# Issuing 64-row matmuls in turns for two heads, one in each row half of the array, and laying out the PSUM pools anew

## The chip, the core and the metric

The kernel runs on one core of one Trainium2 chip. The metric is the device time of one execution in microseconds (us), as the median of several runs of the same program. TensorE is called PE here, VectorE DVE, ScalarE ACT, GpSimd POOL and SyncE SP, as the profile calls them.

## What is computed

Two layers of a decoder trunk on 512 positions with 1024 features. Each layer is a gated feed-forward block, a mixer and a second feed-forward block, each on a normalised and modulated input. The mixer projects its input once and runs three head groups on it: a gated linear recurrence (HGRN2), sparse attention whose keys an indexer selects, and a state-space scan (SSD). Cut to what matters here:

```python
def token_mixing(h, w_in, w_out, ...):
    (hq, hf, hi, hg, aq, ak, av, iq, ik, iw, sz, sxbc, sdt) = jnp.split(h @ w_in, offsets, axis=-1)
    o_a = hgrn2_mixer(hq, hf, hi, hg, lb, hg_norm_g)             # 4 heads of 64
    o_b = dsa_mixer(aq, ak, av, iq, ik, iw, kn_g, kn_b)          # 4 heads of 64, 8 index heads of 64
    o_c = mamba2_mixer(sz, sxbc, sdt, ...)                       # 8 heads of 64, state 128
    return jnp.concatenate([o_a, o_b, o_c], axis=-1) @ w_out

def dsa_mixer(...):                                              # for each block of 128 queries
    logits = jax.nn.relu(jnp.einsum('bthd,bsd->bths', qib, k_idx))
    score = jnp.einsum('bths,bth->bts', logits, wib)             # causal, future keys at -1e30
    _, sel = lax.top_k(score, n_keep)                            # n_keep = 128
    s = jnp.einsum('bthd,btkd->bhtk', qb, k_sel) * ATT_DIM ** -0.5
    return jnp.einsum('bhtk,btkd->bthd', jax.nn.softmax(s), v_sel)

def reference(x, c, ...):
    for l in range(2):
        x = x + 0.5 * g1 * swiglu(modulate(rms_norm(x)), w_ffn_gu[l, 0], w_ffn_down[l, 0])
        x = x + g2 * token_mixing(modulate(rms_norm(x)), w_in[l], w_out[l], ...)
        x = x + 0.5 * g3 * swiglu(modulate(rms_norm(x)), w_ffn_gu[l, 1], w_ffn_down[l, 1])
    return rms_norm(x, final_norm_g)
```

## The kernel before

The residual stream lies feature-major in eight tiles of 128 features by 512 positions. Large products are made in fp32r by splitting each operand into a high and a low part and adding three matmuls (`mm3`, L304 to L307); weights arrive by DMA in SP's queue as `wraw`, ACT makes the high part `whi` (L300) and DVE the low part `wlo` (L301). The two feed-forward blocks of a layer make gate and up products (`pg`, `pu`) per 128 hidden features, and then the down product `pd`.

The mixer (from L443) projects some outputs feature-major, as `pf` in `fm` (24 matmuls of 512 columns each), and others time-major, as `pt` in `tm_group` (96 matmuls of 256 columns for each of the groups `winV`, `winG`, `winC0`, `winC1`). Its parts are generators, which `zipped` (L729) advances in the order of positions given by hand (`ZD`, `ZH`, `ZQ`, `ZC`, `ZG`, `ZS`, `ZA`). The order on each engine is set when the kernel is built: a scheduler with a time model of its own moves instructions among those that are ready, by priority, where the pools have a free buffer. On the chip each engine runs its list in that order.

The parts that the change touches:
- `topk` (L536) makes the index scores. For each query block j from 1 to 3 and each of 8 index heads, a matmul `ipl` of 64 contracted rows (L543) goes through a relu on ACT (L545) and is added to `iacc` on DVE (L548, L550). Then 16 rounds of MAX8 (L559) and MATCH_REPLACE8 (L560) per block pick 128 keys.
- `attend(j)` (L743) takes each of the four heads in turn: score matmul `apl` of 64 rows (L750), softmax on DVE and ACT (L754 to L757), transposes `apt` (L761), a copy `pT` on ACT (L763), and the product with the values `apo` (L765).
- `hgrn` (L613) makes the diagonal `ldg` (L645) and seven levels of the chunk's scores. A level is two differences on DVE (L656, L657), an exponential on ACT (L658), two products on POOL (L659, L660), matmuls `lsc` of 64 rows (L667) and a COPY_PREDICATED into `asc` on DVE (L669). Then the states `hst` are carried over four blocks (`hps` L704, `hpo` L695 and L698).
- `ssd` follows with `pxs`, `pcb`, `prow`, `pyd`, `pst` and `pyo`, and the output product is `po` (L305 to L307 again), whose input `pyt` (L917) transposes.

A head of 64 features lies in rows 0 to 63 or 64 to 127 of its tile, so the matmuls of even heads use the upper half of the array's rows and those of odd heads the lower half. An fp32 matmul is two passes and has two records in the trace; a transpose has one.

[...] Before, `psmm` holds three buffers (`mm`, L70), and `pssm` holds three for `sm` (L73) and two for `hm` (L76), each of one bank:

```python
        pm = pool("psmm", 3, space=bass.MemoryType.PSUM)
        pq = pool("pssm", 2, space=bass.MemoryType.PSUM)
```

Of the kernel before, what the change touches and what calls it, by code (L numbers as in the profile page):

```python
# [11 lines left out]
F32 = mybir.dt.float32  # L12
# [6 lines left out]
P = 128  # L19
D = 1024  # L20
S = 512
# [33 lines left out]
def body(nc, tc, A):  # L55
    ctx = ExitStack()
    with ctx:
# [5 lines left out]
        pm = pool("psmm", 3, space=bass.MemoryType.PSUM)  # L63
        pq = pool("pssm", 2, space=bass.MemoryType.PSUM)
# [189 lines left out]
        def lead(l, i, ws, ps):  # L254
# [8 lines left out]
            pb = sm("pb", (P, 2))  # L263
            with tc.manual_schedule(engines={mybir.EngineType.PE}):
                for k, (xh, xl) in enumerate(ahead):
                    if k == KR[0]:
                        rs = rstd(range(NB), sm)
                    if k == KR[1]:
                        rb = act("C", "rb")
                        ACT.activation(rb, spread_rows(rs, sm), AF.Copy)  # L270
                    for (wh, wl, _), p in zip(ws, ps):
                        mm3(p, wh[:, blk(k)], wl[:, blk(k)], xh, xl, k == 0, k == NF - 1)
# [38 lines left out]
        def begin(pre):  # L311
            with tc.high_priority(0):
                for f in range(NF):
                    sumsq(f, tag="A", eng=V)
                rs = rstd(range(NB), hm)
                rb = act("A", "rb")
                ACT.activation(rb, spread_rows(rs, hm), AF.Copy)
# [10 lines left out]
                for step in SEQ:  # L328
# [11 lines left out]
                    else:  # L340
                        j = len(W)
                        pre[j] = mm("pg"), sm("pu")
# [22 lines left out]
        def ffn(l, w, side, nxt):  # L365
# [5 lines left out]
            else:  # L371
                pre[0] = mm("pg"), sm("pu")
                hh, hl, sb, rb = lead(l, i, [weights(A["wgu"][l, w, 0, g], 1024, True) for g in range(2)], pre[0])
            for hf in range(2):
                ah, al = [], []
                for jj in range(n):
# [3 lines left out]
                    else:  # L380
                        pg, pu = mm("pg"), sm("pu")
# [24 lines left out]
                for f in range(NF):  # L406
# [15 lines left out]
                    else:  # L422
                        with tc.manual_schedule(engines={mybir.EngineType.PE}):
# [5 lines left out]
                            rs = rstd((0, 1), sm)  # L429
                            down(half(1), KT[0], KT[1])  # L430
                            prb = spread_rows(rs, sm)
                            down(half(1), KT[1], n)
                            update(f, pd, gate, None, hf, half(1))
                            rs = rstd((2, 3), sm)
# [3 lines left out]
                            finish(half(1), spread_rows(rs, sm))  # L438
# [5 lines left out]
        def mixer(l, nxt):  # L444
# [68 lines left out]
            for src in (ik, ak):  # L513
# [10 lines left out]
                ps = sm("kTp")  # L524
# [11 lines left out]
            def topk():  # L536
                for j in range(1, NB):
                    n = (j + 1) * P
                    acc = act("A", "iacc")
                    for h in range(IH):  # L540
                        pl = sm("ipl")
                        ph = slice((h % 2) * 64, (h % 2) * 64 + 64)
                        PE.matmul(pl[:, :n], iqr[h // 2][ph, blk(j)], ikT[ph, :n], start=True, stop=True)  # L543
                        rl = act("A", "irl")
                        ACT.activation(rl[:, :n], pl[:, :n], AF.Relu)  # L545
                        w = iw[:, j, h:h + 1]
                        if h == 0:
                            V.tensor_scalar(acc[:, :n], rl[:, :n], w, None, op0=OP.mult)  # L548
                        else:
                            V.scalar_tensor_tensor(acc[:, :n], rl[:, :n], w, acc[:, :n], op0=OP.mult, op1=OP.add)  # L550
# [54 lines left out]

            def hgrn():
# [33 lines left out]
                for par in range(2):  # L640
                    for f in range(2):
                        ps = hm("ldg", (P, NB, P))
                        ph = slice(par * 64, par * 64 + 64)
                        for b in range(NB):
                            PE.matmul(ps[:, b], kf[f][ph, blk(b)], q[f][ph, blk(b)], start=True, stop=True)  # L645
                        V.tensor_tensor(Asc[par][f], ps, ident[:, None, :].to_broadcast([P, NB, P]), op=OP.mult)
                yield
                for li, m in enumerate(LEVELS):
# [13 lines left out]
                    for par in range(2):  # L662
                        ph = slice(par * 64, par * 64 + 64)
                        for f in range(2):
                            ps = hm("lsc")
                            for b in range(NB):
                                PE.matmul(ps[:, blk(b)], xl[f][ph, blk(b)], xl[f][ph, blk(b)],  # L667
                                          start=True, stop=True)
                            V.copy_predicated(v4(Asc[par][f].rearrange("p b t -> p (b t)"))[:, :, 1],  # L669
                                              masks[:, li].rearrange("p (g m) -> p g m", m=m), v4(ps)[:, :, 1])  # L670
                    yield
                kd = [act("B", "kd", shape=(P, NB, P)) for _ in range(2)]
                for f in range(2):
# [5 lines left out]
                    ps = hm("pkd", (P, NB, P))  # L679
# [10 lines left out]
                for b in range(NB):  # L690
                    po = hm("hpo", (P, 2, P))
# [9 lines left out]
                    if b < NB - 1:  # L701
                        for f in range(2):
                            pk = hm("hps", (P, P))
# [39 lines left out]
            def attend(j):  # L743
                n = (j + 1) * P
                po = sm("apo", (P, AH, 64))
                rsum = sp.tile([P, AH], F32, name="rsum")
                for h in range(AH):
                    ph = slice((h % 2) * 64, (h % 2) * 64 + 64)
                    pl = sm("apl")
                    PE.matmul(pl[:, :n], aqr[h // 2][ph, blk(j)], akT[ph, :n], start=True, stop=True)  # L750
                    pe = act("A", "pexp")
                    mx = sp.tile([P, 1], F32, name="amx", bufs=4)
                    bias = negm if j == 0 else selb[j][:, :n]
                    V.tensor_tensor_reduce(pe[:, :n], pl[:, :n], bias, 1.0, GONE, op0=OP.add, op1=OP.max,  # L754
                                           accum_out=mx)
                    V.tensor_scalar(mx, mx, -0.125, None, op0=OP.mult)
                    ACT.activation(pe[:, :n], pe[:, :n], AF.Exp, scale=0.125, bias=mx,  # L757
# [322 lines left out]
```

## Time and profile before

| | us |
|---|---|
| median of 3 runs | 2137.86 |
| lowest and highest | 2137.69, 2138.67 |
| span of the profiled execution | 2136.6 |
| PE busy | 2084.7 (98%) |
| DVE busy | 1304.8 (61%) |
| ACT busy | 817.7 (38%) |

The profiled span lies 1.3 us under the median. Busy time is what an engine's own instructions cover; a matmul's record lasts longer than the distance to the next one, since matmuls are pipelined, so what a matmul costs is read from start to start.

### The profile page before, as it was taken

The page shows a single profiled execution, that of the slowest core. Times are in us where ns is not written, and L with a number is a line of the kernel's source. Part 1 is how long each engine was busy: PE and PEld are TensorE (multiplying, and loading weights), DVE is VectorE, ACT ScalarE, POOL GpSimd, SP SyncE. Part 2 cuts the span into 40 slices and gives each one's busy share as a digit, 9 for nine tenths or more (in the row PEclk, how much of TensorE's full clock was granted, in tenths as well). Part 3 has the DMA queues.
Part 4 walks back from the last instruction along what each step waited for, and adds up shares of the span by engine and source line. Part 5 has one row for each costly group of instructions (what it writes and reads, how often), then busy time and mean ns, then how long its engine had stood idle before and what let it go on. Part 6 is the DMA issues. An engine that isn't in the chain of part 4 may idle for free.

```text
span 2136.6 us, 26813 instructions
## 1 busy us (share of the span) xinstructions
PE 2084.7 (98%) x10201; PEld 1724.8 (81%) x10201; DVE 1304.8 (61%) x2540; ACT 817.7 (38%) x1245; POOL 201.1 (9%) x178
## 2 busy tenths in 40 slices
PE   4999999999999999999999999999999999999998
PEld 3888888887888788888888888888779877888886
DVE  8766564769986877433476743357699775333333
ACT  4422223455564532222342222234655644222233
POOL 4000000112221200000100000011123120000001
PEclk9999999999999999999999999999999999999999
DMA  8556563432110367432346743233311023233322
GB/s 307 204 194 234 179 209 89 128 104 65 58 31 15 121 204 263 129 99 84 94 139 222 273 155 99 78 106 110 94 55 43 16 72 99 90 88 114 94 84 73
DMA packets 103537, 262.51 MB, mean 123 GB/s; under 512 B 12272, under 2 KB 14960, under 8 KB 103408
## 3 DMA queue, kind: packets, MB, share of 16 engines
q1 hardware_dynamic: 100016, 256.60, 37.6%
q10 hardware_dynamic: 3392, 4.20, 0.7%
q8 instruction: 80, 1.31, 0.3%
q14 instruction: 49, 0.40, 0.1%
HBM read 255.50 MB, written 2.10 MB: 121 GB/s over the span
## 4 chain that ended last, share of the span: by engine, by line
PE 94%; DVE 4%; DMA 1%; issue 1%; ACT 1%; SPq 0%; DVEq 0%; ACTq 0%
PE pd L305 7%; PE pd L307 7%; PE pd L306 7%; PE pg L305 7%; PE pu L307 7%; PE pg L306 7%; PE pu L305 7%; PE pu L306 7%; PE pg L307 7%; PE pf L305 3%; PE pf L307 3%; PE pf L306 3%; PE lsc L667 3%; PE pt L469 2%; PE pt L471 2%; PE pt L470 2%
## 5 line engine op out<-in xcount | busy, mean ns | idle before, releaser
L300 ACT ACTIVATE whi<-wraw 128x1024 fp32r<-128x1024 f32 (+2 forms) x374 | 356.7, 957 | 978.3 <-issue 335.2
L301 DVE TENSOR_TENSOR wlo<-wraw,whi 128x1024 fp32r<-128x1024 f32 (+2 forms) x374 | 412.3, 1103 | 389.1 <-ACT whi L300 387.7
L306 PE MATMUL pd<-alo,whi 128*128 128x512 f32 (+1 forms) x715 | 275.8, 386 | 0.0
L307 PE MATMUL pd<-ahi,wlo 128*128 128x512 f32 (+1 forms) x715 | 275.8, 386 | 0.0
L305 PE MATMUL pd<-ahi,whi 128*128 128x512 f32 (+1 forms) x715 | 275.5, 386 | 0.0
L307 PE MATMUL pu<-hhi,wlo 128*128 128x512 f32 x664 | 258.6, 390 | 1.6 <-DVE wlo L301 1.6
L305 PE MATMUL pu<-hhi,whi 128*128 128x512 f32 x664 | 258.7, 390 | 0.2
L305 PE MATMUL pg<-hhi,whi 128*128 128x512 f32 x664 | 258.6, 390 | 0.0
L306 PE MATMUL pu<-hlo,whi 128*128 128x512 f32 x664 | 258.4, 389 | 0.0
L307 PE MATMUL pg<-hhi,wlo 128*128 128x512 f32 x664 | 258.3, 389 | 0.0
L306 PE MATMUL pg<-hlo,whi 128*128 128x512 f32 x664 | 258.3, 389 | 0.0
L160 DVE SCALAR_TENSOR_TENSOR adaw<-adaw,crow 128x512 f32<-128x512 f32 x288 | 193.2, 710 | 5.2 <-DMA adaw<-wada 5.0
L199 POOL TENSOR_TENSOR sq<-sq 128x512 f32<-128x512 f32 x36 | 53.9, 1496 | 1421.4 <-ACT sq L195 1421.2
L396 DVE TENSOR_TENSOR a<-a,pu 128x512 f32<-128x512 f32 x85 | 58.4, 687 | 201.6 <-PE pu L307 201.6
L307 PEld LDWEIGHTS pd<-ahi,wlo 128*128 128x128 f32 x715 | 134.3, 188 | 27.1
L306 PEld LDWEIGHTS pd<-alo,whi 128*128 128x128 f32 x715 | 134.3, 188 | 27.0
L305 PEld LDWEIGHTS pd<-ahi,whi 128*128 128x128 f32 x715 | 134.3, 188 | 27.0
L307 PEld LDWEIGHTS pu<-hhi,wlo 128*128 128x128 f32 x664 | 124.7, 188 | 28.7 <-DVE wlo L301 2.9
L305 PEld LDWEIGHTS pu<-hhi,whi 128*128 128x128 f32 x664 | 124.6, 188 | 27.1 <-ACT whi L300 1.5
L307 PEld LDWEIGHTS pg<-hhi,wlo 128*128 128x128 f32 x664 | 124.6, 188 | 26.0
L305 PEld LDWEIGHTS pg<-hhi,whi 128*128 128x128 f32 x664 | 124.7, 188 | 25.8
L306 PEld LDWEIGHTS pu<-hlo,whi 128*128 128x128 f32 x664 | 124.6, 188 | 25.8
(305 smaller groups left out, 3361.1 us busy)
## 6 DMA issues: line engine op xcount, KB each, us to landing
wraw<-wgu SPq DMA_DIRECT2D x176, 512.0 KB, 3.6
adaw<-wada SPq DMA_DIRECT2D x288, 256.0 KB, 5.0
wraw<-wdn SPq DMA_DIRECT2D x64, 384.0 KB, 3.1
wraw<-wdn SPq DMA_DIRECT2D x64, 320.0 KB, 2.9
wraw<-winF SPq DMA_DIRECT2D x36, 512.0 KB, 3.6
wraw<-woutB SPq DMA_DIRECT2D x16, 384.0 KB, 3.1
wraw<-winC SPq DMA_DIRECT2D x8, 512.0 KB, 3.6
rope<-rraw ACTq DMA_DIRECT2D x48, 64.0 KB, 3.8
```

The lines of the kernel that those rows point to most:

```text
L160: V.scalar_tensor_tensor(raw, raw, 1.0, crow[:, h], op0=OP.mult, op1=OP.mult, accum_out=part[:, c, h:h + 1])
L199: (eng if f < NF - 1 else V).tensor_add(ssq_t["t"][:, h], ssq_t["t"][:, h], sq[:, h])
L300: ACT.activation(hi, raw, AF.Copy)
L301: V.tensor_sub(lo, raw, hi.bitcast(F32))
L305: PE.matmul(ps, wh, xh, start=first, stop=False)
L306: PE.matmul(ps, wh, xl, start=False, stop=False)
L307: PE.matmul(ps, wl, xh, start=False, stop=last)
L396: V.tensor_mul(a, a, pu)
L469: PE.matmul(o, hh[kk][:, blk(b)], wh[:, wk], start=first, stop=False, **g)
L470: PE.matmul(o, hl[kk][:, blk(b)], wh[:, wk], start=False, stop=False, **g)
L471: PE.matmul(o, hh[kk][:, blk(b)], wl[:, wk], start=False, stop=last, **g)
L667: PE.matmul(ps[:, blk(b)], xl[f][ph, blk(b)], xl[f][ph, blk(b)], start=True, stop=True)
```

## The change

Three edits, all in the order and the homes of existing work; no operation is added or removed.

1. **Pools.** `psmm` has four one-bank buffers, and a new pool `pspair` has two buffers of two banks each (`pair`). `sm` and `hm` are gone: what they held goes to `mm`, or to a pair where two heads or gate and up share one.
2. **Pairs.** `topk`, `ldg`, `lsc` (through the new helper `head_pair`) and `attend` issue the matmuls of an even and an odd head in turns, the even head's result in the first bank of a pair, the odd head's in the second. In the attention the softmax of both heads follows, then both heads' transposes into a second pair, then both copies and value products.
3. **Feed-forward.** `pg` and `pu` are the two halves of one pair, so two gate-and-up steps can be held and not three.

```diff
-        pm = pool("psmm", 3, space=bass.MemoryType.PSUM)
-        pq = pool("pssm", 2, space=bass.MemoryType.PSUM)
+        pm = pool("psmm", 4, space=bass.MemoryType.PSUM)
+        pq = pool("pspair", 2, space=bass.MemoryType.PSUM)
...
-        def sm(name, shape=(P, S)):
-            return pq.tile(list(shape), F32, name=name, tag="sm", bufs=3)
-
-        def hm(name, shape=(P, S)):
-            return pq.tile(list(shape), F32, name=name, tag="hm", bufs=2)
+        def pair(name):
+            return pq.tile([P, 2, S], F32, name=name, tag="pair")
...
-                        pg, pu = mm("pg"), sm("pu")
+                        pgu = pair("pgu")
+                        pg, pu = pgu[:, 0], pgu[:, 1]
...
+                    for h2 in range(IH // 2):
+                        pl = pair("ipl")
+                        for u in range(2):
+                            ph = slice(u * 64, u * 64 + 64)
+                            PE.matmul(pl[:, u, :n], iqr[h2][ph, blk(j)], ikT[ph, :n], start=True, stop=True)
...
+            def head_pair(name, kx, qx):
+                ps = pair(name)
+                for b in range(NB):
+                    for u in range(2):
+                        ph = slice(u * 64, u * 64 + 64)
+                        PE.matmul(ps[:, u, blk(b)], kx[ph, blk(b)], qx[ph, blk(b)], start=True, stop=True)
+                return ps
...
-                    for par in range(2):
-                        ph = slice(par * 64, par * 64 + 64)
-                        for f in range(2):
-                            ps = hm("lsc")
-                            for b in range(NB):
-                                PE.matmul(ps[:, blk(b)], xl[f][ph, blk(b)], xl[f][ph, blk(b)],
-                                          start=True, stop=True)
+                    for f in range(2):
+                        ps = head_pair("lsc", xl[f], xl[f])
+                        for par in range(2):
...
-                    ps = hm("pkd", (P, NB, P))
+                    ps = mm("pkd", (P, NB, P))
...
-                for h in range(AH):
-                    ph = slice((h % 2) * 64, (h % 2) * 64 + 64)
-                    pl = sm("apl")
-                    PE.matmul(pl[:, :n], aqr[h // 2][ph, blk(j)], akT[ph, :n], start=True, stop=True)
+                for h2 in range(AH // 2):
+                    pl = pair("apl")
+                    for u in range(2):
+                        ph = slice(u * 64, u * 64 + 64)
+                        PE.matmul(pl[:, u, :n], aqr[h2][ph, blk(j)], akT[ph, :n], start=True, stop=True)
...
-                    pt = sm("apt")
-                    for s_ in range(j + 1):
-                        PE.transpose(pt[:, blk(s_)], pe[:, blk(s_)], ident)
+                    pt = pair("apt")
+                    for u in range(2):
+                        for s_ in range(j + 1):
+                            PE.transpose(pt[:, u, blk(s_)], pes[u][:, blk(s_)], ident)
```

The scheduler gives another order with it. In the whole program the 672 passes of 64 rows stand in 86 uninterrupted rows on PE before and in 42 now, and the halves alternate within each. Two places of the mixer of layer 0 follow; layer 1 has the same pattern. The columns are line, operation, result<-operands and shape.

Place 1, PE, where the first levels of the recurrence (`lsc`) and the first transposes of the attention (`apt`) stand; `pf` is the feature-major projection. Before:

```order
L307 MATMUL pf<-hhi,wlo 128x512
L305 MATMUL pf<-hhi,whi 128x512
L761 MATMUL apt<-ident,pexp 128x128
L667 MATMUL lsc<-lev 128x128 x4
L306 MATMUL pf<-hlo,whi 128x512
L307 MATMUL pf<-hhi,wlo 128x512
L667 MATMUL lsc<-lev 128x128 x4
L305 MATMUL pf<-hhi,whi 128x512
```

And now, PE, from the last index scores `ipl` on:

```order
L304 MATMUL pf<-hhi,wlo 128x512
L547 MATMUL ipl<-kT,rope 128x512 x6
L618 MATMUL lsc<-lev 128x128 x64
L762 MATMUL apl<-kT,rope 128x128 x2
L777 MATMUL apt<-ident,pexp 128x128
L762 MATMUL apl<-kT,rope 128x128 x2
L777 MATMUL apt<-ident,pexp 128x128
L782 MATMUL apo<-kv,pT 128x64
L302 MATMUL pf<-hhi,whi 128x512
```

The `lsc` matmuls, which stood four at a time between projections, are now 64 in a row: eight groups of eight, four levels, with no projection among them.

Place 2, PE, where the time-major projections `pt` stand. Before:

```order
L471 MATMUL pt<-wlo,hhi 128x256
L469 MATMUL pt<-whi,hhi 128x256
L470 MATMUL pt<-whi,hlo 128x256
L667 MATMUL lsc<-lev 128x128 x3
L761 MATMUL apt<-ident,pexp 128x128 x2
L667 MATMUL lsc<-lev 128x128 x5
L471 MATMUL pt<-wlo,hhi 128x256
```

And now, PE, at the first `pt` matmuls after `winV`; `hps` and `hpo` carry the recurrence's state, `pacs` is the first product of the scan:

```order
L714 MATMUL hps<-vv,kd 128x128
L705 MATMUL hpo<-hst,hq 128x128
L708 MATMUL hpo<-vv,asc 128x64 x2
L826 MATMUL pacs<-da,cst 128x32 x2
L826 MATMUL pacs<-da,ones 128x32
L472 MATMUL pt<-whi,hhi 128x256
L473 MATMUL pt<-whi,hlo 128x256
L474 MATMUL pt<-wlo,hhi 128x256
```

The 288 `pt` matmuls of `winG`, `winC0` and `winC1`, which stood among the levels and the attention, now follow both, as one block, and the scan follows the block.

Between the two places the second half of the attention (`attend(2)` and `attend(3)`) now stands with little but itself on PE:

```order
L762 MATMUL apl<-kT,rope 128x384 x2
L777 MATMUL apt<-ident,pexp 128x128 x3
L762 MATMUL apl<-kT,rope 128x384 x2
L777 MATMUL apt<-ident,pexp 128x128 x3
L782 MATMUL apo<-kv,pT 128x64 x6
L777 MATMUL apt<-ident,pexp 128x128 x3
L762 MATMUL apl<-kT,rope 128x512 x2
L777 MATMUL apt<-ident,pexp 128x128 x3
```

Four pairs of heads stand there one behind the other; before, `pt` matmuls stood between such steps. The order of the feed-forward blocks' matmuls is unchanged but for the rows around each normalisation.

## Rows read from the trace of the kernel before

**Rows 1.** The page's busy times and its chain of waits, by engine

```profile
PE 2084.7 (98%) x10201; PEld 1724.8 (81%) x10201; DVE 1304.8 (61%) x2540; ACT 817.7 (38%) x1245; POOL 201.1 (9%) x178
...
PE 94%; DVE 4%; DMA 1%; issue 1%; ACT 1%; SPq 0%; DVEq 0%; ACTq 0%
```

**Rows 2.** Stretch 500 to 620: length, PE, PEld, DVE, ACT, POOL busy, PEclk, DMA

```profile
500.00:620.00 120.00, 119.97 (x762) 98.86 (x761) 117.33 (x291) 68.58 (x115) 35.34 (x37) 1.00 0.18 51
```

**Rows 3.** Groups of 64-row matmuls: xcount | busy us, mean ns | idle before

```profile
L667 PE MATMUL lsc<-lev 64*128 64x128 f32 x448 | 60.9, 280 | 0.0
L543 PE MATMUL ipl<-kT,rope 64*128 64x256 f32 (+2 forms) x96 | 33.5, 520 | 0.0
L750 PE MATMUL apl<-kT,rope 64*128 64x128 f32 (+3 forms) x64 | 25.7, 482 | 0.0
L645 PE MATMUL ldg<-hq,kf 64*128 64x128 f32 x64 | 8.7, 278 | 0.0
```

**Rows 4.** Timeline of PE where two kinds of 64-row matmul meet: start, duration

```profile
601.46 0.48 PE L750 MATMUL apl<-kT,rope 64*128 64x256 f32 x1
601.47 0.49 PE L667 MATMUL lsc<-lev 64*128 64x128 f32 x2
```

**Rows 5.** Timeline of PE around a 64-row pair that stands alone

```profile
608.00 0.28 PE L471 MATMUL pt<-wlo,hhi 128*128 128x256 f32 x1
608.12 0.38 PE L761 MATMUL apt<-ident,pexp 128*128 128x128 f32 x2
608.44 0.70 PE L750 MATMUL apl<-kT,rope 64*128 64x256 f32 x2
609.06 0.39 PE L469 MATMUL pt<-whi,hhi 128*128 128x256 f32 x1
```

**Rows 6.** Timeline of PE at both ends of layer 0's mixer stretch

```profile
486.68 0.70 PE L543 MATMUL ipl<-kT,rope 64*128 64x256 f32 x4
...
715.11 0.39 PE L307 MATMUL po<-yhi,wlo 128*128 128x512 f32 x1
715.34 0.39 PE L305 MATMUL pg<-xhi,whi 128*128 128x512 f32 x1
```

**Rows 7.** Groups of DVE's instructions in the stretch 486 to 716

```profile
L301 DVE TENSOR_TENSOR wlo<-wraw,whi 128x1024 fp32r<-128x1024 f32 (+1 forms) x23 | 26.4, 1151 | 4.5 <-ACT whi L300 4.5
L559 DVE MAX8 m<-iacc 128x8 f32<-128x256 f32 (+2 forms) x48 | 26.2, 548 | 0.2
L560 DVE MATCH_REPLACE8 iacc<-m,iacc 128x256 f32<-128x256 f32 (+2 forms) x48 | 26.1, 543 | 0.0
L585 DVE SCALAR_TENSOR_TENSOR xbc<-xraw,vec,xbc 128x511 f32<-128x511 f32 (+2 forms) x18 | 14.7, 816 | 0.0
L669 DVE COPY_PREDICATED asc<-masks,lsc 128x256 f32<-128x256 uint8 x28 | 14.3, 510 | 0.9 <-PE lsc L667 0.9
L550 DVE SCALAR_TENSOR_TENSOR iacc<-irl,kv,iacc 128x384 f32<-128x384 f32 (+2 forms) x20 | 13.7, 685 | 0.2
...
L656 DVE TENSOR_TENSOR lev<-bf 128x256 f32<-128x256 f32 x14 | 6.4, 460 | 0.0
```

**Rows 8.** Groups of DVE's instructions in the stretch 500 to 620, first and last

```profile
L560 DVE MATCH_REPLACE8 iacc<-m,iacc 128x384 f32<-128x384 f32 (+2 forms) x47 | 25.7, 546 | 0.0
...
L812 DVE COPY acs<-pacs 128x32 f32<-128x32 f32 x1 | 0.2, 165 | 0.0
```

**Rows 9.** Timeline: one head's softmax and the transposes that follow it

```profile
635.93 0.56 DVE L754 CUSTOM_DVE_ANT_0 pexp<-apl,iacc 128x384 f32<-128x384 f32 x1 [0.93 <-PE apl L750]
...
639.32 0.49 PE L761 MATMUL apt<-ident,pexp 128*128 128x128 f32 x3
```

**Rows 10.** Timeline: the first transposes of two successive chunks of the scan

```profile
638.43 0.60 PE L822 MATMUL pxs<-ident,xbc 128*128 128x128 f32 x4
...
647.90 0.66 PE L822 MATMUL pxs<-ident,xbc 128*128 128x128 f32 x4
```

**Rows 11.** Timeline of PE near the start of the program, in a sparsely filled stretch

```profile
35.56 0.63 PE L307 MATMUL pg<-hhi,fw 128*128 128x512 f32 x1
```

More of the change, by code (lines that the diff above doesn't have):

```diff
@@ L266, in lead @@
                     if k == KR[0]:
-                        rs = rstd(range(NB), sm)
+                        rs = rstd(range(NB), mm)
                     if k == KR[1]:
                         rb = act("C", "rb")
-                        ACT.activation(rb, spread_rows(rs, sm), AF.Copy)
+                        ACT.activation(rb, spread_rows(rs, mm), AF.Copy)
                     for (wh, wl, _), p in zip(ws, ps):
@@ L314, in begin @@
                     sumsq(f, tag="A", eng=V)
-                rs = rstd(range(NB), hm)
+                rs = rstd(range(NB), mm)
                 rb = act("A", "rb")
-                ACT.activation(rb, spread_rows(rs, hm), AF.Copy)
+                ACT.activation(rb, spread_rows(rs, mm), AF.Copy)
                 hh, hl = first_tiles()
@@ L539, in topk @@
                     acc = act("A", "iacc")
-                    for h in range(IH):
-                        pl = sm("ipl")
-                        ph = slice((h % 2) * 64, (h % 2) * 64 + 64)
[L543 to L550, printed above, removed]
+                    for h2 in range(IH // 2):
[4 more added lines that the diff above has]
+                        for u in range(2):
+                            h = 2 * h2 + u
+                            rl = act("A", "irl")
+                            ACT.activation(rl[:, :n], pl[:, u, :n], AF.Relu)
+                            w = iw[:, j, h:h + 1]
+                            if h == 0:
+                                V.tensor_scalar(acc[:, :n], rl[:, :n], w, None, op0=OP.mult)
+                            else:
+                                V.scalar_tensor_tensor(acc[:, :n], rl[:, :n], w, acc[:, :n], op0=OP.mult,
+                                                       op1=OP.add)
                     V.tensor_tensor(acc[:, blk(j)], acc[:, blk(j)], negm, op=OP.add)
@@ L744, in attend @@
                 n = (j + 1) * P
-                po = sm("apo", (P, AH, 64))
+                po = mm("apo", (P, AH, 64))
                 rsum = sp.tile([P, AH], F32, name="rsum")
-                for h in range(AH):
-                    ph = slice((h % 2) * 64, (h % 2) * 64 + 64)
-                    pl = sm("apl")
-                    PE.matmul(pl[:, :n], aqr[h // 2][ph, blk(j)], akT[ph, :n], start=True, stop=True)
[L751 to L757, printed above, removed]
-                                   accum_out=rsum[:, h:h + 1])
-                    pt = sm("apt")
-                    for s_ in range(j + 1):
-                        PE.transpose(pt[:, blk(s_)], pe[:, blk(s_)], ident)
-                    pT = act("A", "pT")
-                    ACT.activation(pT[:, :n], pt[:, :n], AF.Copy)
-                    for s_ in range(j + 1):
-                        PE.matmul(po[:, h], pT[:, blk(s_)], av[:, s_], start=s_ == 0, stop=s_ == j)
@@ L954, in load @@
                     return (*held, f % 4 * 2)
[L955 removed]
+                yield from project((0, 1), mm, load, None, False)
             def flagged(name, g):
```

61 lines of the change are left out of this document (41 added, 20 removed).

## The prediction, made before the changed kernel ran

> **What bounds the kernel now.** I read the busy times and the chain of waits first: PE is busy 98% of the span and carries 94% of the chain, with DVE at 61% [rows 1]. So far a saving on PE is a saving in time. The average hides the mixer, though, so the next view is its busy times by stretch. From 500 to 620 PE is busy 119.97 of 120 us, and DVE 117.33 of 120 at the same time [rows 2]: two engines are full at once there. DVE's work is mostly the selection of keys, which nobody can use before it is over; PE is full only because projections that need nothing from DVE stand between the matmuls that do. [...] What the change is worth is decided here: by who still feeds PE while DVE works.
>
> The frame of the sum is layer 0's mixer from its first index matmuls at 486.68 to the first gate matmul of the next block at 715.34, 228.7 us [rows 6]. The same instructions stand between these two points after the change, so I build that time anew. All is set against the profiled span of 2136.6; the median is 1.3 above it.
>
> **What pairing takes from PE.** There are 448 + 96 + 64 + 64 = 672 passes of 64 rows [rows 3]. One pass of 256 columns alone is recorded with 0.48 us [rows 4] and two with 0.70 [rows 5], so a further one costs 0.22, or 0.86 ns a column. By the shapes the 672 passes stream 122,880 columns: 106 us, 53 per layer. If the two halves run side by side, half of it goes: 26 per layer. That they do so is to be seen already: an `apl` starts at 601.46 and an `lsc` at 601.47, 0.01 apart, where one after the other would leave 0.22 [rows 4]. Each uninterrupted row also costs an entry and an exit. The two transposes at 608.12 stream until about 608.34, `apl` starts at 608.44, and the next `pt` 0.62 later although two passes stream in 0.44 [rows 5]: 0.10 + 0.18 = 0.28. The order shows 43 such rows per layer before and 21 now, so 22 x 0.28 = 6. PE's work per layer falls by some 32 us, from about 225 to 192.
>
> **What the new order costs.** The matmuls keep PE busy only if something stands between them, and that is what has moved. I cut the stretch at the places where the order changes character.
>
> *First part: up to the end of the selection.* On DVE there stand, by the groups of the stretch [rows 7]: MAX8 26.2 and MATCH_REPLACE8 26.1, all of them; `iacc` 13.7, with 12 more short steps for first heads, causal bias and threshold that I take at 0.5 each, 6; 28 differences at 0.44 (6.4 for 14, and a second line like it), 12.4; 20 of the 28 COPY_PREDICATED at 0.51, 10.2; 12 of the `xbc` steps at 0.82, 9.8; 7 `wlo` at 1.15, 8.1; and the maxima of the first two attention blocks, 8 at about 0.55, 4.4. That is 117. For the short rest (value loads, scans, `ldg` products) I allow 14, an estimate: 131. Neighbours on DVE overlap: the 25 groups of the stretch 500 to 620, from MATCH_REPLACE8 with 25.7 to COPY with 0.2 [rows 8], add up to 137.8 us of durations in 117.33 busy [rows 2], a factor of 0.85. So DVE needs 131 x 0.85 = 112 us, in one go.
>
> PE has for that time only 117 `pf` matmuls at 0.23 [rows 6], 27 us; 128 pairs-to-be of 64 rows, 40 us in series, 20 in pairs; and about 5 for the rest: 52. And it can't run ahead: the 64 `lsc` in a row stand in front of everything else, and each group of eight waits for differences on DVE, which are spread through the selection, then for ACT and POOL. PE waits at the head of its list and the projections behind it wait as well. So 60 us of idle time, where there was none.
>
> *Second part: the late half of the attention and the end of the recurrence.* PE's own work is 48 `pf` (11 us), the paired 64-row rows (6), 36 transposes, 42 narrow and 11 state matmuls and their changes of kind (17): 34. Between scores and transposes of one head lay 3.4 us before, from 635.93 to 639.32 [rows 9], filled with other work. Now four pairs of `attend(2)` and `attend(3)` stand one behind another and each shows about that once, partly more since two heads go through DVE and ACT, partly less since a second pair is in flight: 4 x 4 = 16. Together 50; from 40, if the next pair covers half, to 62, if the state steps of the recurrence stand bare too.
>
> *Third part:* 288 `pt` at 0.12 [rows 5], 35. It is dense, but it comes after DVE's work and no longer beside it.
>
> *Fourth part: the scan.* One chunk's first transposes lie 9.5 us behind another's [rows 10], with other work between. Four chunks and the last one's end: 42, against PE's own 34.5. *Fifth:* the output products, 144 at 0.23 and the transposes, 36, with the waits at the norm 40.
>
> Sum per layer: 112 + 50 + 35 + 42 + 40 = 279, against 228.7: **+50**. Bounds: the first part 108 to 124 (the short rest at 9, or DVE waiting for scores on top), the second 40 to 62, the third 35 to 37, the last two 74 to 98: +28 to +92.
>
> *The clock.* [...] The first part is sparse now. Most of what it would lengthen is hidden by DVE; I put in 4 per layer, from 0 to 15.
>
> *Feed-forward.* Gate and up lose a buffer, three pairs become two. One step of PE is 48 matmuls, 11 us at 0.23, far longer than the `wlo` step of 1.15 [rows 7] or any other single step that reads its result, so one pair in reserve is enough: nothing inside, and 0 to 5 for the three normalisations; I take 3.
>
> Total: 2136.6 + 2 x (50 + 4) + 3 = 2248, and with 1.3 for the median **2249**; I say 2250.
>
> The trace has DVE full while PE is full [rows 2], which speaks against gaining anything in this stretch. [...]
>
> **Rivals.**
> 1. *It does what it is for* (faster). PE stays fed and keeps the 32 us per layer less some waits of 4: 2138 - 2 x 28 = 2082. For it: 98% on PE [rows 1]. Against it: 288 `pt` have left the stretch where DVE is full. It decides at an idle time of 32 per layer; I have 60 in the first part alone. 6%, of which one ends near the old time.
> 2. *The same loss, but mild.* DVE's work overlaps better, the 48 `pf` of the second part and the next pair cover the attention, and the scan runs at PE's pace: 104 + 42 + 35 + 35 + 36 = 252, or 23 more than 228.7, with 2 x 23: 2184. 14%.
> 3. [...] 15%. [...]
> 4. *The halves don't run side by side.* PE's rows keep 26 us more; 20 of it vanish in the idle of the first part, 6 in the second show: 2250 + 2 x 6 = 2262. Against it: 0.01 between two starts [rows 4]. 3%.
>
> **How the numbers follow.** My forecast has 62%. The range reaches down to rival 2 and up to rival 3, and takes in most of the bounds (2 x 28 to 2 x 92, so 2194 to 2322): 2180 to 2312. Left out are rival 1 and the upper tails. A measurement tells 0.2%, some 4 us, from no change. Faster 0.05 and same 0.03 come from rival 1 and the mildest end of rival 2; slower 0.92.
>
> **What would show it.** PE's busy share falls to some 90% while DVE's time is unchanged. A stretch of about 110 us after the first `ldg` shows DVE near full and PE about half, idle ahead of `lsc` and released by POOL, and idle ahead of `apt` released by ACT. After it a dense block of `pt` with DVE nearly idle. Within a pair the two halves start a few ns apart, and the groups of 64-row matmuls are half as long. I'm wrong in kind if PE stays full in that stretch, wrong in size if the idle time lies elsewhere: in the feed-forward blocks, or in the scan.

## The result, and the profile after

The changed kernel takes 2310.6 us (median of 4 runs, 2308.8 to 2314.3) against 2138.2 for the kernel before: a ratio of 1.081, with a 95% interval of 1.079 to 1.082. It is 172 us slower. The profiled execution has a span of 2312.5, against 2136.6.

The page of the changed kernel, busy times, DVE and the granted clock in 40 slices, and the chain of waits by engine:

```profile
PE 2124.8 (92%) x10201; PEld 1752.9 (76%) x10201; DVE 1313.2 (57%) x2540; ACT 822.1 (36%) x1241; POOL 201.4 (9%) x178
...
DVE  8765656659734765633475743374794467333333
...
PEclk9999999897579999999999999998956999999999
...
PE 82%; DVE 12%; ACT 3%; issue 2%; DMA 1%; POOL 0%; SPq 0%; DVEq 0%; ACTq 0%; POOLq 0%
```

PE and DVE run as many instructions as before [rows 1], but PE is busy 92% of a longer span, its part in the chain falls from 94% to 82%, and DVE's rises from 4% to 12%. Nearly all of the loss lies in the two mixers, where the clock's row has its dips. PE's busy time has even grown, by 40 us, although the four groups of 64-row matmuls take 99.8 us and not 128.8 [rows 3]: at the lower clock, granted 0.941 in the mean and not 0.998, the other matmuls take longer (`apo` 358 ns each and not 266, `apt` 394 and not 278).

Busy times of the changed kernel by stretch, layer 0, cut at the marks of the prediction's parts (columns: stretch, length, PE, PEld, DVE, ACT, POOL, clock, DMA share, GB/s). The last row is the stretch at the keys' transposes, ahead of the first mark:

```profile
505.40:531.10 25.70, 25.21 (x136) 18.08 (x136) 23.31 (x42) 14.52 (x27) 8.21 (x8) 1.00 0.26 82
531.10:618.10 87.00, 52.49 (x280) 37.02 (x278) 85.73 (x244) 32.49 (x62) 17.87 (x19) 0.63 0.08 22
618.10:683.30 65.20, 52.57 (x272) 41.94 (x272) 25.59 (x65) 26.74 (x49) 8.15 (x11) 0.69 0.05 17
683.30:720.80 37.50, 37.50 (x297) 37.50 (x298) 9.55 (x14) 10.45 (x17) 6.14 (x6) 0.94 0.18 57
720.80:805.50 84.70, 77.98 (x416) 65.65 (x415) 59.11 (x93) 42.20 (x97) 16.16 (x12) 0.94 0.16 50
428.60:443.00 14.40, 2.35 (x12) 1.78 (x11) 10.34 (x50) 4.96 (x9) 1.01 (x1) 0.61 0.13 37
```

From 531 to 618 the selection runs: DVE is full, PE has 52 of 87 us, at a clock of 0.63. In the kernel before PE was full in the same company [rows 2]. The marks themselves, from the timelines of PE and DVE (start, duration): the first `ldg`, the last MATCH_REPLACE8 and the first gate matmul of the next block:

```profile
505.39 1.16 PE L618 MATMUL ldg<-hq,kf 64*128 64x128 f32 x16
...
617.47 0.68 DVE L567 MATCH_REPLACE8 iacc<-m,iacc 128x512 f32<-128x512 f32 x1
...
805.42 0.39 PE L302 MATMUL pgu<-xhi,whi 128*128 128x512 f32 x1
```

The selection ends at 618.15. In the kernel before it ended with this row:

```profile
617.03 0.68 DVE L560 MATCH_REPLACE8 iacc<-m,iacc 128x512 f32<-128x512 f32 x1
```

That is 617.71, so at this mark the two kernels stand level. But by then the changed kernel has done 48 `pf` and 275 `pt` matmuls fewer; 187 us of mixer are still to come, and before it was 98 [rows 6].

PE's longest waits in the changed kernel among those that the kernel before doesn't have (what waited and for whom: us in all, times, longest):

```profile
PE apt L777 <- ACT pexp L771: 45.7, 10, 7.0
PE kTp L529 <- ACT kr L526: 24.0, 4, 10.3
PE lsc L618 <- DVE asc L678: 19.9, 12, 3.1
...
PE pkd L691 <- POOL kf L688: 9.6, 2, 4.8
```

Two of the four are as the prediction had them: transposes that wait for the softmax, and rows of `lsc` that wait. The `lsc` wait, though, is for DVE's COPY_PREDICATED, which frees a pair, and not for POOL's products. And `kTp`, the keys' transposes, is in none of its steps. Timeline of PE there, start, duration and in brackets the idle time before:

```profile
439.17 1.12 PE L529 MATMUL kTp<-ident,kr 128*128 128x128 f32 x4 [10.29 <-ACT kr L526]
442.04 1.11 PE L529 MATMUL kTp<-ident,kr 128*128 128x128 f32 x4 [1.76 <-ACT kr L526]
442.81 0.78 PE L302 MATMUL pf<-hhi,whi 128*128 128x512 f32 x1
443.38 0.63 PE L303 MATMUL pf<-hlo,whi 128*128 128x512 f32 x1
443.81 0.63 PE L304 MATMUL pf<-hhi,wlo 128*128 128x512 f32 x1
```

The projections behind `kTp` wait 10 us with it and then start 0.43 apart, where 0.23 is usual [rows 6]; the granted clock is 0.50 from 443.30 to 445.00.

That the halves do run side by side is plain. Timeline of the changed kernel, 16 passes of `lsc` at the full clock (granted 1.00) and at the lower one (0.50):

```profile
548.50 1.16 PE L618 MATMUL lsc<-lev 64*128 64x128 f32 x16 [0.26 <-ACT irl L551]
552.76 2.08 PE L618 MATMUL lsc<-lev 64*128 64x128 f32 x16 [3.09 <-DVE asc L678]
```

At 0.11 a pass, half of the 0.22 between one pass of 256 columns [rows 4] and two [rows 5], 16 in a series would need more than 1.7, an estimate; the first row has 1.16. The second has the wait for the pair and the price of the clock in one line.

### The profile page after: what moved, and what is told of

Its sections match the earlier page's. It is cut to its first block, busy times and chain, and to the rows that moved or that the text cites. A ratio compares the mean times of both kernels' runs of the same rounds, so it can differ in the third digit from the quotient of the medians.

```text
span 2312.5 us, 26800 instructions
## 1 busy us (share of the span) xinstructions
PE 2124.8 (92%) x10201; PEld 1752.9 (76%) x10201; DVE 1313.2 (57%) x2540; ACT 822.1 (36%) x1241; POOL 201.4 (9%) x178
## 4 chain that ended last, share of the span: by engine, by line
PE 82%; DVE 12%; ACT 3%; issue 2%; DMA 1%; POOL 0%; SPq 0%; DVEq 0%; ACTq 0%; POOLq 0%
PE pgu L303 13%; PE pgu L302 13%; PE pgu L304 13%; PE pd L302 7%; PE pd L303 7%; PE pd L304 7%; PE pf L302 2%; PE pf L303 2%; PE pf L304 2%; DVE iacc L567 2%; PE pt L473 2%; PE pt L472 2%; PE pt L474 2%; DVE m L566 2%; PE po L303 1%
## 5 line engine op out<-in xcount | busy, mean ns | idle before, releaser
L303 PE MATMUL pgu<-hlo,whi 128*128 128x512 f32 x1312 | 511.4, 390 | 5.4 <-DVE hlo L286 5.4
L302 PE MATMUL pgu<-hhi,whi 128*128 128x512 f32 x1312 | 511.1, 390 | 2.7 <-DVE u L394 2.7
L304 PE MATMUL pgu<-hhi,wlo 128*128 128x512 f32 x1312 | 510.3, 389 | 0.0
L303 PEld LDWEIGHTS pgu<-hlo,whi 128*128 128x128 f32 x1312 | 246.2, 188 | 59.7 <-DVE hlo L286 9.3
L302 PEld LDWEIGHTS pgu<-hhi,whi 128*128 128x128 f32 x1312 | 246.3, 188 | 55.0 <-DVE u L394 4.0
L304 PEld LDWEIGHTS pgu<-hhi,wlo 128*128 128x128 f32 x1312 | 246.3, 188 | 51.1
L302 PE MATMUL pf<-hhi,whi 128*128 128x512 f32 x256 | 107.3, 419 | 0.0
L304 PE MATMUL pf<-hhi,wlo 128*128 128x512 f32 x256 | 104.7, 409 | 0.0
L303 PE MATMUL pf<-hlo,whi 128*128 128x512 f32 x256 | 104.7, 409 | 0.0
L473 PE MATMUL pt<-whi,hlo 128*128 128x256 f32 (+1 forms) x320 | 91.8, 289 | 6.5 <-DVE hlo L286 6.3
```

The costliest lines, as they stand in the source:

```text
L302: PE.matmul(ps, wh, xh, start=first, stop=False)
L303: PE.matmul(ps, wh, xl, start=False, stop=False)
L304: PE.matmul(ps, wl, xh, start=False, stop=last)
L473: PE.matmul(o, hl[kk][:, blk(b)], wh[:, wk], start=False, stop=False, **g)
```

## The experiments

Theory A: the loss comes from the order, and the order from the pools. Theory B: it comes from working in pairs, which makes two heads wait for each other. Twelve kernels were run; each time stands against 2138.3 to 2138.8 for the kernel before on the same chip, and what is said against the changed kernel stands against its 2310.6.

**1. The new pools alone.** Heads one by one as before, `mm` with four banks, `sm` with four in place of the two pairs.

```diff
-                pre[0] = mm("pg"), sm("pu")
+                pre[0] = sm("pg"), sm("pu")
...
-                po = sm("apo", (P, AH, 64))
+                po = mm("apo", (P, AH, 64))
...
-                            ps = hm("lsc")
+                            ps = sm("lsc")
```

> The new pools without the pairs: four banks mm, and four one-bank buffers in place of the two pairs; the matmuls stand head by head as before the change. Theory A (the loss comes from the order, and the order from the pools: kTp, pkd, hpo, hps, apo and pyt now share mm with the projections, whose buffers are handed out in program order): the same long rows of lsc and the same block of 288 pt, so about as slow as the changed kernel, 2290 to 2340 us. Theory B (the loss comes from working in pairs: two heads must both be through DVE and ACT before PE goes on, and only two pairs are held): 2140 to 2180 us.

Measured: 2338.9 us. Theory A. The pools alone cost 200 us; with the pairs in them it is 28 less.

**2. The pairs of `ldg` and `lsc` alone, in the old pools.**

```diff
-                    for par in range(2):
-                        ph = slice(par * 64, par * 64 + 64)
-                        for f in range(2):
-                            ps = hm("lsc")
-                            for b in range(NB):
+                    for f in range(2):
+                        pp = [hm("lsc") for _ in range(2)]
+                        for b in range(NB):
+                            for par in range(2):
+                                ph = slice(par * 64, par * 64 + 64)
```

> The pairs without the new pools: ldg and lsc (512 of the 672 passes of 64 rows) alternate between the halves in the two hm banks of the kernel before; all else as before. The projections stay between the groups of eight. Theory A: no loss. PE has 14 us a layer less to stream and about 8 rows fewer to enter; if PE stays fed that is up to 30 us in all, 2108 us, but DVE is full where most lsc stand, so I expect 2120 to 2138. Theory B: each group now holds both banks until DVE has read both, and PE waits for that as it does in the changed kernel: 2150 to 2200.

Measured: 2148.9 us, 0.5% slower than before (0.3 to 0.6%). Neither theory's number, though close to the lower end of theory B's. The pairing does what it says; the group of all `lsc`, before [rows 3] and here:

```profile
L668 PE MATMUL lsc<-lev 64*128 64x128 f32 x448 | 42.1, 295 | 0.0
```

60.9 us have become 42.1. But no time is saved. Stretches of this kernel among the selection:

```profile
540.00:560.00 20.00, 15.97 (x93) 12.06 (x93) 19.77 (x52) 15.01 (x22) 4.52 (x6) 1.00 0.28 80
560.00:580.00 20.00, 20.00 (x171) 18.59 (x173) 19.99 (x57) 14.35 (x23) 4.41 (x5) 0.92 0.18 53
```

DVE is as full as before and PE now has gaps. Where the further 10 us come from I can't show beyond that: the matmuls behind the selection stand in another order too, and the tail is some 3 us longer per layer. Experiment 11 has the same pairs without the 10 us, so the pairs as such don't cost them.

**3. A bank of their own for the small users.** The changed kernel with three banks for `mm` and one for `kTp`, `pkd`, `hpo`, `hps`, `apo` and `pyt`.

```diff
-        pm = pool("psmm", 4, space=bass.MemoryType.PSUM)
+        pm = pool("psmm", 3, space=bass.MemoryType.PSUM)
...
+        def hm(name, shape=(P, S)):
+            return pq.tile(list(shape), F32, name=name, tag="hm", bufs=1)
```

> The changed kernel with one thing taken back: mm has three banks, and the eighth bank is a buffer of its own for kTp, pkd, hpo, hps, apo and pyt. The pairs stay. Theory A: projections stand between the levels and the attention again and no dense block of pt comes after them, so most of the loss goes: 2150 to 2210 us, of which some stays since the hgrn state steps and apo now follow each other through one bank. Theory B: 2270 to 2310, since the pairs are as they were.

Measured: 2216.7 us, 94 less with the pairs as they were: 7 above theory A's range and 53 below theory B's. Of the 78 us that stay, the longest new waits name a part: the first stands behind a late recurrence, the second is for a pair to come free, the third for the softmax (PE's waits in this kernel). The rest is open.

```profile
PE pyt L937 <- DVE yhg L965: 13.5, 2, 6.8
...
PE lsc L621 <- DVE asc L681: 11.9, 9, 2.9
PE apt L780 <- ACT pexp L774: 10.4, 7, 3.2
```

**4. The halves apart.** The changed kernel with the loops of `head_pair` exchanged.

```diff
-                for b in range(NB):
-                    for u in range(2):
+                for u in range(2):
+                    for b in range(NB):
```

> The changed kernel with lsc and ldg issued one half after the other into the same pairs, so that the halves overlap only where they meet; the order on all engines is otherwise the same. PE then streams 14 us a layer more at the full clock. Theory A (PE idles there and the saving of the pairs is hidden): within 10 us of the changed kernel, 2305 to 2320. If the pairs' saving still counts: 28 us or, at the lower clock, up to 50 more, 2338 to 2360.

Measured: 2317.6 us, 7 more. The group of all `lsc`, in the changed kernel and here, and the first 16 passes of `ldg` here, behind `pf` that start 0.23 apart (in the changed kernel 1.16 behind the same `pf` at the same distance, at a granted clock of 1.00):

```profile
L618 PE MATMUL lsc<-lev 64*128 64x128 f32 x448 | 48.5, 379 | 20.2 <-DVE asc L678 19.9 <-ACT irl L551 0.3
...
L618 PE MATMUL lsc<-lev 64*128 64x128 f32 x448 | 68.0, 382 | 10.6 <-DVE asc L678 10.6
...
506.02 1.71 PE L618 MATMUL ldg<-hq,kf 64*128 64x128 f32 x16
```

In the new order the alternation takes 19.5 us from the busy time of `lsc`, and 7 of them show; 9.6 come back as idle time ahead of `lsc`.

**5. The gates' projections earlier.**

```diff
-ZD, ZH, ZQ, ZC, ZG = (0.18, 0.59), (0.04, 0.86), (0.04, 0.63), (0.06, 0.79), (0.89, 0.94)
+ZD, ZH, ZQ, ZC, ZG = (0.18, 0.59), (0.04, 0.86), (0.04, 0.63), (0.06, 0.79), (0.30, 0.60)
```

> The changed kernel with one pair of numbers altered: the gates' projections (the 288 pt) take positions 0.30 to 0.60 of the mixer in the order by hand, no longer 0.89 to 0.94. With it some 250 pt stand among ipl, lsc and the first attention blocks, and none after the recurrence; the third part, 37 us, goes. If the loss is that PE has too little to do while DVE selects (theory A), the 35 us of pt disappear in that idle time, and the clock stays up there: 70 to 100 us less, 2210 to 2240. If DVE and the pairs set the length wherever pt stands (theory B), or pt only pushes the chain back: 2290 to 2320.

Measured: 2277.7 us, 33 less: between the theories. The block of `pt` is gone, but what is put ahead is lacking later. Two stretches of this kernel:

```profile
580.00:600.00 20.00, 8.11 (x59) 6.57 (x58) 20.00 (x58) 10.19 (x19) 3.96 (x4) 0.64 0.18 52
...
620.00:640.00 20.00, 13.25 (x64) 9.48 (x64) 9.08 (x32) 9.94 (x21) 3.27 (x4) 0.58 0.07 21
```

The attention and the recurrence still stand bare: `apt` waits for the softmax for 33.0 us in all (45.7 in the changed kernel), and the clock is low there, 0.58 in the second stretch.

**6. `kTp` in half a pair.**

```diff
-                ps = mm("kTp")
+                ps = pair("kTp")[:, 0]
```

> The changed kernel with one tile moved: kTp, the transposes of the keys, lives in half a pair and not in mm. By the order this gives back only the place before the first index scores (projections stand between pt and kTp again); the order behind is the same. The wait of 10 us at kTp and the slow matmuls around it cost 18 us a layer by the two traces, so 2 x 18 less: 2274. If that idle time is only passed on to the DVE-bound part behind it, nothing is gained: 2300 to 2312.

Measured: 2265.8 us, 45 less. This one home is a quarter of the loss. From 420 to 460 PE is full and the clock at 1.00 again, and in layer 0 the selection ends at 599.28, 19 us earlier:

```profile
420.00:440.00 20.00, 20.00 (x138) 18.41 (x138) 15.15 (x30) 7.57 (x11) 4.37 (x3) 1.00 0.44 128
440.00:460.00 20.00, 20.00 (x118) 17.62 (x118) 9.94 (x35) 8.71 (x13) 0.00 (x0) 1.00 0.32 94
```

**7. Added work to hold the clock.**

```diff
                     pt = pair("apt")
+                    for _ in range(10):
+                        PE.matmul(pt[:, 0, :P], ident, ident, start=True, stop=True)
```

> The changed kernel with added work: ahead of the transposes of each attention pair, 10 fp32 products of the identity with itself go into the tile that the transposes overwrite. [...] If the lower granted clock from 540 to 650 costs much of what the prediction missed, keeping PE busier holds the clock and gives back 10 to 25 us: 2285 to 2300. If the clock is hidden behind DVE, the added work costs 0 to 16 x 1.5: 2310 to 2335.

Measured: 2290.0 us, 21 less with 160 passes more per layer. Stretches of this kernel behind the end of the selection:

```profile
600.00:620.00 20.00, 17.48 (x107) 15.04 (x106) 19.04 (x55) 8.38 (x19) 3.29 (x4) 0.74 0.01 1
620.00:640.00 20.00, 18.03 (x128) 14.98 (x127) 6.04 (x25) 7.05 (x18) 0.00 (x0) 1.00 0.00 1
```

From 620 to 640 the clock is 1.00, and in the changed kernel it was 0.50 there:

```profile
600.00:620.00 20.00, 12.22 (x62) 8.76 (x62) 18.97 (x53) 6.87 (x13) 2.36 (x3) 0.59 0.00 0
620.00:640.00 20.00, 15.06 (x52) 9.42 (x52) 3.53 (x18) 5.76 (x16) 0.94 (x2) 0.50 0.00 1
```

So the added work is worth 10 us per layer, net of what it takes itself. The gain lies behind the selection: from its end to the last `po`, layer 0 takes 168.9 us and not 187.1, layer 1 168.9 and not 180.6. The likely reason is the clock, 1.00 and not 0.50 from 620 to 640. It isn't shown alone, since with the added work the scheduler also puts the transposes of both heads one behind the other.

**8. Low parts of weights on POOL**, with the pairs of experiment 2.

```diff
-                V.tensor_sub(lo, raw, hi.bitcast(F32))
+                eng.tensor_sub(lo, raw, hi.bitcast(F32))
...
-                wh, wl = weights(A["winF"][l, c], 1024)
+                wh, wl = weights(A["winF"][l, c], 1024, eng=GP if c >= 10 else V)
```

> The old pools with ldg and lsc in pairs (2148.9 us) and 14 of the low parts wlo of each mixer's weights moved from DVE to POOL (those of the convolution and the gates, 1.15 us each on DVE, where they stand among the selection; POOL is 10% busy). If DVE being full there is what kept the saving of the pairs from showing, DVE is 15 us shorter per layer and 10 to 14 us of PE's saving shows per layer: 2118 to 2135. If something else eats it (waits on pexp, the late recurrence), 2145 to 2165.

Measured: 2183.6 us, 35 more than experiment 2 and above both expected ranges. It tells nothing on DVE, since the move itself costs more than DVE could gain. The group on POOL, which was 1.15 us each on DVE [rows 7]:

```profile
L301 POOL TENSOR_TENSOR wlo<-wraw,whi 128x1024 fp32r<-128x1024 f32 x28 | 70.9, 2532 | 85.7 <-ACT whi L300 85.7
```

At 2.53 us each they stand between the levels' products in POOL's list, and the order on PE is another one too.

**9. `apo` in `mm`, nothing else**, in the kernel before.

```diff
-                po = sm("apo", (P, AH, 64))
+                po = mm("apo", (P, AH, 64))
```

> The kernel before with one word altered: the attention's accumulator apo takes its bank from mm, where the projections pf and pt take theirs, and no longer from sm. Nothing is paired, and no bank is added. apo holds its buffer from the first head of a query block to the last, and mm hands its buffers out in program order, so the projections that come later in the program wait for it. In the order the 288 pt go behind the levels and the attention, as in the changed kernel; the projections ahead of kTp keep their place. Theory A: this one home makes most of the loss that lies behind the first index scores, 2 x 45 to 2 x 70 over the kernel before: 2228 to 2278. Theory B (the pairs make it): 2138 to 2160.

Measured: 2245.1 us, in theory A's range. One word costs 107 us, where the whole change costs 172. In layer 0 the selection ends at 605.37, 12 us earlier than before, so the loss lies wholly behind it. Stretches of this kernel:

```profile
560.00:580.00 20.00, 15.52 (x74) 13.27 (x73) 20.00 (x55) 7.37 (x13) 7.90 (x8) 0.56 0.04 16
580.00:600.00 20.00, 19.51 (x76) 15.49 (x76) 19.36 (x56) 5.71 (x15) 4.99 (x4) 0.50 0.00 1
600.00:620.00 20.00, 20.00 (x77) 15.78 (x75) 10.70 (x34) 6.17 (x16) 0.61 (x3) 0.50 0.00 0
```

With the projections gone behind, only small fp32 matmuls stand from 580 to 620 (`lsc`, `apo`, `apl`, `hpo`, `hps` and a few transposes), and they run at 0.50 although PE has work nearly the whole time.

**10. `kTp` in `mm`, nothing else**, in the kernel before.

```diff
-                ps = sm("kTp")
+                ps = mm("kTp")
```

> The kernel before with the keys' transposes kTp in mm and no longer in sm. In the order the 48 pf that stood among the pt ahead of kTp go behind it; the rest stays as it was. Theory A: the wait of some 10 us at kTp and the matmuls around it appear as in the changed kernel, 2 x 15 to 2 x 22: 2168 to 2182. If what is missed there is made up for later, since DVE bounds the part behind: 2138 to 2150.

Measured: 2179.7 us, 41 more, at the upper end of theory A; the wait is the same as in the changed kernel:

```profile
PE kTp L526 <- ACT kr L523: 20.4, 2, 10.2
```

Nothing of it is made up for later. Experiments 9 and 10 add up to 148 us without a single pair. They weren't run together, and the new pools alone cost 200 (experiment 1), so some 50 us of the pools' price have no single home shown for them.

**11. All the pairs in the old pools.** As experiment 2, with the index heads in twos and the attention by pairs of heads in `sm`.

```diff
-                for h in range(AH):
-                    ph = slice((h % 2) * 64, (h % 2) * 64 + 64)
-                    pl = sm("apl")
+                for h2 in range(AH // 2):
+                    pl = [sm("apl") for _ in range(2)]
```

> The old pools with all the pairs: ldg and lsc as in the second experiment (2148.9 us), the index heads in twos, and the attention by pairs of heads, scores, softmax, transposes and products of both heads together, in the sm banks. Theory A: 2140 to 2165, since projections still stand between the steps. Theory B (both heads must be through DVE and ACT before PE goes on): 2180 to 2230.

Measured: 2139.3 us, a ratio of 1.0005 (0.9995 to 1.0015): no change, and theory B is out for the pairs that form. Not all do: in the scheduler's order `lsc` and `ldg` alternate, but half of the `apl` and most `ipl` still stand head by head. The page, the groups of `ipl` and `apl` (33.5 and 25.7 before [rows 3]), and a cut at 617, where the selection of the kernel before ends (here it ends at 621.46):

```profile
PE 2072.0 (97%) x10201; PEld 1706.9 (80%) x10201; DVE 1308.1 (61%) x2540; ACT 832.2 (39%) x1257; POOL 203.9 (10%) x178
...
L545 PE MATMUL ipl<-kT,rope 64*128 64x256 f32 (+2 forms) x96 | 35.1, 524 | 1.5 <-ACT irl L547 1.5
...
L756 PE MATMUL apl<-kT,rope 64*128 64x128 f32 (+3 forms) x64 | 19.3, 482 | 0.0
...
495.00:617.00 122.00, 115.92 (x750) 89.35 (x748) 119.36 (x295) 77.54 (x125) 34.61 (x36) 0.97 0.16 47
617.00:716.00 99.00, 96.60 (x596) 82.03 (x595) 72.72 (x137) 53.00 (x122) 22.26 (x20) 1.00 0.14 42
```

PE has 13 us less to do than before [rows 1], and has them as gaps: 6 of the 122 us up to 617, where DVE is busy 119. That pairs don't cost time where all of them form is shown from the other side: with the same small users in `mm`, the changed kernel is 28 us faster than experiment 1, which has no pairs.

**12. Half of the selection**, in the changed kernel; the other half is left out, so fewer keys are kept.

```diff
-                    for r in range(TOPK // 8):
+                    for r in range(TOPK // 16):
```

> The changed kernel with 8 rounds of the selection per query block and not 16, so that half of MAX8 and MATCH_REPLACE8 is left out and fewer keys are kept: 26 us of DVE's durations less per layer, some 22 us of its time. If DVE's length sets the part from the first index scores to the end of the selection, the time falls by about 2 x 22: 2266, or somewhat more or less by the order, 2255 to 2280. If the waits on the pairs' buffers and on the softmax set it: 2295 to 2312.

Measured: 2288.6 us, between the two expected ranges: 22 less, half of what a part bound by DVE alone would give. In layer 0 the selection ends 38 us earlier (580.49 against 618.15), but the last `po` starts only 14 earlier (790.78 against 805.20). So DVE's length is one half of the matter. What takes its place (PE's waits in this kernel):

```profile
PE apt L777 <- ACT pexp L771: 34.0, 10, 6.9
...
PE pkd L691 <- POOL kf L688: 18.2, 2, 9.1
```

And a stretch of it:

```profile
580.00:600.00 20.00, 16.95 (x78) 11.88 (x77) 7.08 (x26) 6.22 (x18) 2.82 (x4) 0.50 0.00 1
```

The wait at `pkd` has nearly doubled, and from 580 to 600 the clock is 0.50 with DVE down to 7.08 of 20. DVE doesn't set the pace there; that the chain of the attention and the levels does is read from these waits, not shown by a run.

No kernel among these beats the one before; the best, experiment 11, equals it.

## Why the prediction came out as it did, point by point

- **What bounds, and that DVE's fullness forbids a gain:** right. Experiments 2 and 11 are that statement: the pairs take a third from `lsc` and 7 and 13 us from PE's busy time, and the time is longer or the same. DVE's largest work in the mixer is the selection, 52.3 us a layer [rows 7].
- **What pairing takes from PE, 32 per layer:** the kind is right, the size isn't reached. In experiment 11 the three groups that pair in part or in full, `lsc`, `ldg` and `apl`, fall from 95.3 [rows 3] to 64.6 us in both layers together, but PE's busy time falls by 13 only, and the runs don't show what takes up the rest. In the changed kernel it hardly matters, since PE is idle there: taking the alternation away costs 7 us (experiment 4).
- **The order as the cause of the loss:** right, shown by experiments 1, 3, 9 and 10. What the prediction didn't say is why the order is another one. It is the homes (experiment 1): `apo` and the recurrence's tiles in the projections' pool, whose buffers go out in program order. Experiment 9 shows it for `apo` and experiment 10 for `kTp`; for the recurrence's tiles no run shows it alone.
- **The first part, 112 per layer:** 505.39 to 618.15, 112.8, with DVE busy for 109.0 of it. The sum over DVE's groups and the factor 0.85 hold. PE's work was put at 52 and is 77.7 (25.21 + 52.49), the larger part of it at a clock of 0.63, hidden behind DVE as the prediction said. That DVE alone sets it is only half true (experiment 12). The wait of `lsc` is for DVE, which frees the pairs, and not for POOL.
- **The second part, 50:** 65. Here lies one error. PE's own work there was put at 34; the row from 618.10 to 683.30 shows 52.57 busy at a clock of 0.69. 34 divided by 0.69 is 49, an estimate, so the 15 that are missing are the clock's for the most part; PE's idle time, 12.6 us, is no longer than the 16 that were put in for waits. The clock was in the sum with 4 per layer, from 0 to 15; no run shows this term. What the runs show is a clock of 0.63 in the first part from 531 on and of 0.69 in the second, and 10 us per layer that experiment 7 took back.
- **The third part, 35, and the last two, 82:** 37.5 and 84.7.
- **The frame:** this is the step that failed most. The prediction began its sum at the first index matmuls and let everything ahead of them stand, as "the same instructions stand between these two points". They do, nearly (3 `pf` and 4 passes of `ipl` are on the other side; the first `ipl` of the kernel before already stand at 447.16). But the point itself moved: in the changed kernel it is 505.39 and not 486.68 [rows 6]. Of the projections that stood ahead of `kTp`, 48 `pf` and 68 `pt` stand behind it now, so PE is idle for 10.29 us where it had them to do; I read the order from the frame's start on. 19 per layer by the traces, 41 to 45 in all by experiments 10 and 6.
- **Together:** layer 0's mixer ends 90 us later (805.42 against 715.34), of which 19 lie ahead of the frame and 71 in it, where 54 were forecast; layer 1's costs 84. The feed-forward blocks cost 2 in all, 3 were forecast. So 2250 is 61 too low: 38 from the frame's start and the rest, an argument from the parts above, from the clock and small excesses. The measured 2310.6 lies inside the stated 2180 to 2312 by 1.4 us, and that is luck: the upper end was drawn up to rival 3, and the delay ahead of the frame was in no term and no bound.
- **The rivals:** the first two, a gain and a mild loss, are out by the time. The third, on the clock, is right that it falls: to 0.63 and 0.69 in the two parts, where it was 1.00 before. But the second part grew by 15 only, and 19 came from a place that no rival named. The 0.63 near the start [rows 11] has no reading of the granted clock beside it: the views print 1.00 there, but the first reading in that trace is at 37.29 us; in the changed kernel the same 0.63 goes with a granted clock of 0.50 (583.50 to 588.80). The fourth is out: 16 passes take 1.16 us in turns and 1.71 one half after the other (experiment 4).

## What to carry to other kernels

Before a gain on the busiest engine is counted, look at the stretch in which it falls: if another engine is full there too, the gain becomes a gap, as in experiment 2 (PE 15.97 of 20 us beside DVE with 19.77). When buffers change their pool, read the order of the whole program and not only of the part that was meant to change; one long-lived tile in the pool of the filler work takes the filler away, as `apo` did for 107 us in experiment 9. And price the parts of a chain with the clock that such a chain has, not with that of the full stretch from which the durations come: here with 0.63 and 0.69, not with 1.00.

## What the runs showed of the hardware

PE was busy without a gap and yet at the lower clock in one run. In experiment 9 PE has gaps from 560 to 580 (15.52 of 20 us busy), at a granted clock of 0.56. From 600 to 620 the clock is still 0.50, with PE busy 20.00 of 20 us on small fp32 matmuls (`lsc`, `apo`, `hpo`) and no projections among them; from 580 to 620 an `lsc` is recorded with 429 ns, and in the kernel before with 280 [rows 3]. From 640 to 660 the clock is 1.00 again, with PE busy 20.00 once more. In the changed kernel the clock is 0.50 to 0.67 in the stretches of 20 us from 540 to 640, with PE busy 8.87 to 15.06 of 20. And added work paid in one run: in experiment 7, 160 more passes per layer made the changed kernel 21 us faster, with the clock at 1.00 from 620 to 640 where it was 0.50.
